# Local attention on one core: the last 512 rows loaded in order of use, and fourteen tiny extra loads

The kernel runs on 1 core of one Trainium2 chip. The metric is the device time of one execution in microseconds (us); the profile's span is some 1.8 us shorter than that time.

Words used below: PE does the matrix products (TensorE); ACT, DVE and POOL are ScalarE, VectorE and GpSimd; SP is SyncE, which here only issues transfers. A transfer (load or store) is issued by POOL or SP and carried out in packets by the 16 DMA engines. Each transfer adds sixteen increments to a semaphore, a counter that others wait on; it has landed when the last one has come. A ratio is a kernel's time over that of the kernel before, with its 95% interval in brackets.

## The reference

q, k and v are float32 of shape (4, 4096, 1536). Attention is taken inside windows of 64 rows.

```python
def reference(q, k, v):
    B, S, D = q.shape
    W = 64
    nw = S // W
    scale = D ** -0.5
    ...                                   # reshape to (B, nw, W, D)
    logits = np.einsum('bnwd,bnud->bnwu', q_w, k_w) * scale
    logits = logits - logits.max(axis=-1, keepdims=True)
    attn = np.exp(logits)
    attn = attn / attn.sum(axis=-1, keepdims=True)
    out = np.einsum('bnwu,bnud->bnwd', attn, v_w)
    return out.reshape(B, S, D).astype(np.float32)
```

There are 302 MB to read and 101 MB to write, and little arithmetic for them.

## The kernel before

The 16384 rows are cut into 32 units of 512 rows. The last unit is cut once more, into parts of 256, 128 and 128 rows, so that little work remains after the last load. Loads convert float32 to float16 and are issued from POOL, as are the stores. Only the first load of q and the last three stores come from SP.

```python
units = [Unit(i * UR, [(0, 4, 2)]) for i in range(N - 1)]
units.append(Unit((N - 1) * UR, [(0, 2, 2), (2, 3, 1), (3, 4, 1)]))
...
qkp = ctx.enter_context(tc.tile_pool(name="qkp", bufs=2))
vp = ctx.enter_context(tc.tile_pool(name="vp", bufs=3))
outp = ctx.enter_context(tc.tile_pool(name="outp", bufs=3))
...
def load(u, i, name):
    lo, hi, R = u.parts[i]
    ...                                   # take the tile, pick the rows
    nc.gpsimd.dma_start(out=dst, in_=rows(src, u.first[i], hi - lo, r))

def load_all(ui, names):
    if ui < N:
        for i in range(len(units[ui].parts)):
            for name in names:
                load(units[ui], i, name)
...
def store(u, i):
    lo, hi, R = u.parts[i]
    nc.gpsimd.dma_start(out=rows(of, u.first[i], hi - lo, R), in_=slots(u.o, lo, hi, R))

for ui, u in enumerate(units):
    for i in range(len(u.parts)):
        last = ui == N - 1 and i == len(u.parts) - 1
        blocks = scores(u, i)             # transposes of q and k on PE, products, exp
        if i == 0:
            load_all(ui + 2, "qk")
        for h, et in blocks:
            values(u, i, h, et, last)     # products with v, scaled; the last part stores itself
        if not last:
            store(u, i)
    load_all(ui + 3, "v")
```

So POOL issues four transfers a unit, always in the order q, k, out, v. Each full one has 3.15 MB on its 4-byte side. v of the last unit is issued before its q and k.

The softmax here doesn't subtract the row's maximum and nothing guards it: scores larger than these inputs give would overflow.

## Time and profile before

| | before |
|---|---|
| median time | 950.28 us (949.49 to 950.36, 3 runs) |
| span of the profiled execution | 948.6 us |
| PE, ACT, DVE busy | 70%, 46%, 45% |
| software DMA queue busy | 100.2% of 16 engines' span |
| landing to landing, one unit, steady state | 29.15 us |

From the page of the kernel before: busy time of each engine, and rows of the span in 40 slices (9 means 90% busy or more), then the DMA queue that holds nearly all bytes.

```profile
span 948.6 us, 12985 instructions
PE 666.8 (70%) x5624; PEld 443.1 (47%) x5624; DVE 426.9 (45%) x491; ACT 434.2 (46%) x612; POOL 83.7 (9%) x139
...
PE   2777776776767867767667677776776767777685
...
DMA  9999999999999999999999999999999999999997
...
q0 software_dynamic: 27232, 249.31, 100.2%
```

No compute engine is near full; the DMA engines are, in every slice but the last. Next, the list of DMA issues (count, KB, median us from issue to landing) and two lines of the list of waits (us in total, times, longest).

```profile
out_dram<-out_sb POOLq DMA_DIRECT2D x31, 3072.0 KB, 41.9
k<-in_k_dram POOLq DMA_DIRECT2D x31, 1536.0 KB, 48.6
v<-in_v_dram POOLq DMA_DIRECT2D x31, 1536.0 KB, 48.7
q<-in_q_dram POOLq DMA_DIRECT2D x30, 1536.0 KB, 53.8
...
```

```profile
POOL out_dram L224 <- issue: 376.6, 28, 14.4
...
PE tp L145 <- DMA k<-in_k_dram: 78.4, 28, 4.3
```

A full transfer takes 7.3 us of the queue, so a latency of 42 to 54 us means six or seven of them stand in line: the queue never lacks work. PE waits 2.8 us for k, 28 times.

What POOL does in steady state (timeline of POOL before: start, us, instruction, idle time before it and what ended that):

```profile
452.97 0.54 POOL L80 DMA_DIRECT2D q<-in_q_dram  x1 [1.34 <-PE tp L145]
463.05 0.54 POOL L80 DMA_DIRECT2D k<-in_k_dram  x1 [9.54 <-DVE xk L151]
476.80 0.71 POOL L224 DMA_DIRECT2D out_dram<-out_sb  x1 [13.21 <-issue]
477.51 0.72 POOL L80 DMA_DIRECT2D v<-in_v_dram  x1
```

POOL waits only for compute there. (The profile names nothing for the store's 13.21 us; that wait ended at 476.25 us, as DVE finished the last piece of the result.) At the end, PE meets the last unit at 918.9 us (timeline of PE before); neither line has a wait in brackets:

```profile
918.93 1.50 PE L145 MATMUL tp<-ident,q 128*128 128x128 f16 x24
920.53 1.20 PE L145 MATMUL tp<-ident,k 128*128 128x128 f16 x16
```

The trace also holds every increment of a DMA's semaphore, sixteen for each transfer. From these I computed when each transfer's first and last increment came. A growing distance between them says that some DMA engines run ahead of others: 0.7 us at 25 us, 9.1 us at 880 us. The trace doesn't name the engine.

### The profile page before, as it was taken

The numbers are of one execution on the slowest core, as the hardware profiler recorded it, in microseconds if no ns is written. First come the engines' busy times: TensorE is split into PE (matmuls) and PEld (weight loads), VectorE is DVE, ScalarE is ACT, GpSimd is POOL, SyncE is SP. The second block draws the span as 40 slices with busy tenths as digits, with TensorE's granted clock in tenths as the row PEclk, the third lists the DMA queues.
The fourth block names the chain that finished last, engine by engine and source line by source line (L and its number), as shares of the span: only waits on it lengthen the run. The fifth ranks groups of instructions, "written<-read, shape, count | busy, mean of one in ns | idle before, by whom it ended". The sixth has DMA issues, their size and how long they took to land. (4 is left out here: it accounts for less than half of the span.)

```text
span 948.6 us, 12985 instructions
## 1 busy us (share of the span) xinstructions
PE 666.8 (70%) x5624; PEld 443.1 (47%) x5624; DVE 426.9 (45%) x491; ACT 434.2 (46%) x612; POOL 83.7 (9%) x139
## 2 busy tenths in 40 slices
PE   2777776776767867767667677776776767777685
PEld 1544554444544545445454354544445534455452
DVE  3545445443454344543445443454434545344442
ACT  2555434444345444454534454435544445453444
POOL 1101110100101011010010100101101001011010
PEclk9999989888899889798988998989988999798798
DMA  9999999999999999999999999999999999999997
GB/s 259 215 234 262 282 280 280 247 253 279 281 278 252 246 282 282 279 263 242 278 281 279 271 241 271 282 279 275 242 263 282 281 277 253 254 279 281 279 258 312
DMA packets 27865, 254.07 MB, mean 268 GB/s; under 512 B 2208, under 2 KB 2208, under 8 KB 11808
## 3 DMA queue, kind: packets, MB, share of 16 engines
q0 software_dynamic: 27232, 249.31, 100.2%
q1 hardware_dynamic: 576, 3.93, 1.1%
q8 instruction: 44, 0.72, 0.3%
q14 instruction: 13, 0.11, 0.0%
HBM read 301.99 MB, written 100.66 MB: 424 GB/s over the span
## 5 line engine op out<-in xcount | busy, mean ns | idle before, releaser
L209 PE MATMUL o<-v,et 128*128 128x512 f16 x762 | 226.8, 402 | 65.6 <-ACT out_sb L215 61.4
L158 PE MATMUL lt<-xq,xk 128*128 128x256 f16 (+1 forms) x1536 | 236.9, 306 | 41.4 <-DVE xk L151 25.9
L151 ACT COPY xk<-tp 128x1024 f16<-128x1024 f16 (+1 forms) x96 | 123.6, 1287 | 255.8 <-PE tp L145 255.8
L217 DVE TENSOR_SCALAR out_sb<-o,rs 128x512 f32<-128x512 f32 x191 | 143.4, 751 | 161.7 <-PE o L209 161.7
L151 DVE COPY xk<-tp 128x1024 f16<-128x1024 f16 (+1 forms) x97 | 123.3, 1271 | 200.7 <-PE tp L145 200.7
L158 PEld LDWEIGHTS <-xk 128*128 128x128 f16 x1536 | 154.1, 110 | 92.3 <-DVE xk L151 39.0
L145 PE MATMUL tp<-ident,k 128*128 128x128 f16 x1536 | 136.4, 245 | 81.7 <-DMA k<-in_k_dram 78.4
L215 ACT ACTIVATE out_sb<-o,rs 128x512 f32<-128x512 f32 x193 | 132.7, 687 | 123.4 <-PE o L209 112.2
L145 PEld LDWEIGHTS <-k 128*128 128x128 f16 x1536 | 118.1, 112 | 94.1 <-DMA k<-in_k_dram 83.2
L209 PEld LDWEIGHTS <-et 128*128 128x128 f16 x762 | 72.7, 99 | 188.1 <-issue 147.5
L151 DVE COPY xq<-tp 128x1024 f16<-128x1024 f16 (+1 forms) x129 | 152.1, 1255 | 5.1 <-PE tp L145 5.0
L145 PE MATMUL tp<-ident,q 128*128 128x128 f16 x1536 | 103.0, 220 | 46.6 <-DVE xq L151 20.8
L145 PEld LDWEIGHTS <-q 128*128 128x128 f16 x1536 | 91.9, 98 | 64.6 <-issue 34.8
L151 ACT COPY xq<-tp 128x1024 f16<-128x1024 f16 x64 | 82.1, 1283 | 83.7 <-PE tp L145 83.7
L184 ACT ACTIVATE et<-lt,zeros 32x128 f16<-32x128 f32 (+1 forms) x256 | 91.8, 359 | 32.9 <-PE lt L158 27.4
L202 DVE RECIPROCAL rs<-sp 128x2 f32<-128x2 f32 (+1 forms) x65 | 10.7, 165 | 133.7 <-PE sp L197 133.7
L224 POOL DMA_DIRECT2D out_dram<-out_sb x33 | 23.2, 704 | 419.0 <-issue 376.6
L80 POOL DMA_DIRECT2D k<-in_k_dram x34 | 18.5, 546 | 352.1 <-PE tp L145 210.4
L197 PE MATMUL sp<-ones,et 128*128 128x1 f16 x254 | 16.0, 166 | 41.1 <-ACT et L184 41.1
L197 PEld LDWEIGHTS <-et 128*128 128x128 f16 x254 | 13.6, 98 | 60.0 <-ACT et L184 50.4
L80 POOL DMA_DIRECT2D q<-in_q_dram x33 | 17.9, 542 | 79.1 <-PE tp L145 58.8
L80 POOL DMA_DIRECT2D v<-in_v_dram x34 | 23.9, 703 | 4.9 <-DMA k<-in_k_dram 4.9
(12 smaller groups left out, 7.6 us busy)
## 6 DMA issues: line engine op xcount, KB each, us to landing
out_dram<-out_sb POOLq DMA_DIRECT2D x31, 3072.0 KB, 41.9
k<-in_k_dram POOLq DMA_DIRECT2D x31, 1536.0 KB, 48.6
v<-in_v_dram POOLq DMA_DIRECT2D x31, 1536.0 KB, 48.7
q<-in_q_dram POOLq DMA_DIRECT2D x30, 1536.0 KB, 53.8
raw<-in_q_dram SPq DMA_DIRECT2D x1, 3072.0 KB, 14.5
out_dram<-out_sb POOLq DMA_DIRECT2D x1, 1536.0 KB, 10.0
v<-in_v_dram POOLq DMA_DIRECT2D x1, 768.0 KB, 46.9
v<-in_v_dram POOLq DMA_DIRECT2D x2, 384.0 KB, 46.4
```

The source lines that it names most:

```text
L80: nc.gpsimd.dma_start(out=dst, in_=rows(src, u.first[i], hi - lo, r))
L145: nc.tensor.transpose(tp[:, (c - c0) * R + r, j, :], src[:, lo + R * j + r, c * P : (c + 1) * P], ident,)
L151: copy(out=dst, in_=tp)
L158: nc.tensor.matmul(lts[h][:, r, :, :], lhsT=kc[:, r, h, :], rhs=qc[:, :, h, :], start=(c == 0 and r == 0), stop=(c == DC - 1), skip_group_ ...
L184: nc.scalar.activation(et[s, :, :, s], lts[h][s, :, :, s], EXP, bias=zeros[s], scale=scale)
L197: nc.tensor.matmul(sp[:, t, 0:1], lhsT=et[:, r, t, :], rhs=ones[:, 0:1], start=(r == 0), stop=(r == R - 1),)
L202: nc.vector.reciprocal(out=rs, in_=sp[:, :, 0])
L209: nc.tensor.matmul(o, lhsT=et[:, r, t, :], rhs=u.v[:, lo + R * h + r, sl], start=(r == 0), stop=(r == R - 1),)
L215: nc.scalar.activation(dst, o, COPY, bias=0.0, scale=rs[:, t : t + 1])
L217: nc.vector.tensor_scalar_mul(dst, o, scalar1=rs[:, t : t + 1])
L224: nc.gpsimd.dma_start(out=rows(of, u.first[i], hi - lo, R), in_=slots(u.o, lo, hi, R))
```

## The change

The intent has two parts. The loads of the last 512 rows are issued in the order in which their parts are computed, so that the first part has all it needs earlier. And in fourteen units from the 15th on, one tiny load of 1 to 15 rows, whose result nobody reads, is put into the stream.

```diff
     def load_all(ui, names):
-        if ui < N:
-            for i in range(len(units[ui].parts)):
-                for name in names:
+        if ui < N - 1:
+            for name in names:
+                load(units[ui], 0, name)
+        elif ui == N - 1 and "q" in names:
+            for i, part in enumerate(("qkv", "qk", "qk")):
+                for name in part:
                     load(units[ui], i, name)
+            load(units[ui], 1, "v")
+            load(units[ui], 2, "v")
@@
+    probe = consts.tile([16, 192], FP32, name="probe")
     for ui, u in enumerate(units):
+        n = ui - 13
+        if 1 <= n <= 15 and n != 8:
+            w = 128 + 4 * n
+            nc.gpsimd.dma_start(out=probe[:n, :w], in_=qf[0:n, :w])
         for i in range(len(u.parts)):
```

In the diff, v of part 0 follows its q and k directly; v of parts 1 and 2 follow after all q and k.

## The prediction

> **What bounds the kernel.** The DMA engines, throughout. The page's DMA row is 9 in 39 of 40 slices and the software queue is busy 100.2% of 16 engines' span; PE is at 70%, ACT 46%, DVE 45%. Landing times (from the trace's semaphore records): in steady state every full load or store (3.15 MB on its 4-byte side) lands about 7.3 us after the one before, a unit of four (q, k, out, v) takes 29.15 us. Compute needs about 24.5 us from k's landing to the store; PE waits 78.4 us for k (list of waits). Issue to landing is 42 to 54 us (list of DMA issues): some 1.6 units stand in the queue.
>
> The end is DMA-bound too. The last load lands at 925.06 us, then the stores with no gap beyond their bytes: 932.40, 939.70, 943.35, 945.21, 945.85, 946.49, 947.13. The chain of waits shows compute from 926 to 944, but each result joins a queue that still holds older stores. The engines are not level: the first to finish a transfer leads the last by 0.7 us at 25 us and 9.1 us at 880 us, growing in jumps of about 1.1 us, near the 44 instruction fetches of 16 KB (about 0.9 us each). The slowest engine, never idle, sets the time.
>
> **What the change does.**
> 1. Last 512 rows: v came ahead of q and k; now each v follows its q and k. Same nine loads, same bytes. Before, part 0's k landed at 917.64 and PE reached that part at 918.7; q and k at about 910 and v at 914 buy nothing, since the slowest engine has the same work left. Last v lands near 925, its use is near 942. Worth 0.
> 2. Fourteen loads of 1 to 15 unused rows, 528 to 752 B a row. By the Trainium skill ("DMA: Bandwidth & Descriptors", why a DMA increments its semaphore by 16) n rows go to n engines and all 16 post the count; before has no such transfer. A 2048 B packet took 85 ns, a 4 B semaphore write 9 to 22 ns; splitting transfers at the end cost 0.02 to 0.06 us each beyond bytes. Estimate 0.035 us each, 0.5 us in all, on the critical DMA stream. Issuing costs POOL about 0.55 us each, hidden.
> 3. New waits on POOL. All probes write one tile, so each should wait for the one before to land; and transfers share eight semaphores in turn, so five a unit instead of four wait for a landing 1.6 units back. POOL should stand some 15 us at each probe; q's issue to landing falls from 53.9 to about 37 us in those units, k's to about 43; probes land in about 29 us. When the wait ends a whole unit (29 us; 20 on the engine furthest ahead) is still queued, so none runs dry: worth 0.
>
> **Predicted: 950.9 us**, range 949.2 to 953.0. Faster by over 2%: 0.01; within 2%: 0.97; slower: 0.02.
>
> **Right if** the DMA row stays 9, full transfers land 7.3 us apart, probes add under 0.1 us each, PE's wait for k is nearly unchanged, the last load lands near 925.5 and the end follows the stores. **Wrong if** POOL's waits run the queue dry (DMA row under 9 from 400 to 860 us, steps over 8 us): slower by up to some per cent; or if odd engine counts turn later transfers onto other engines that move at another rate, or level the lead (at most about 4 us faster); or if a fetch more or less falls on the slowest engine (1.1 us).

## The result, and the profile after

| | before | after |
|---|---|---|
| median time | 950.32 us (949.49 to 950.37, 4 runs) | 951.0 us (950.64 to 951.39, 4 runs) |
| ratio | | 1.0009, 95% interval 0.9992 to 1.0027 |
| span of the profiled execution | 948.6 us | 949.5 us |
| last load lands | 925.06 us | 925.59 us |
| last store lands | 947.13 us | 947.67 us |

A ratio is the mean time of one kernel's runs over that of the other's of the same rounds, so it is not quite the ratio of the medians in the table. The interval includes 1; the difference of 0.7 us is of the size predicted, but these runs alone don't separate it from nothing.

The page after:

```profile
span 949.5 us, 13010 instructions
PE 664.1 (70%) x5624; PEld 436.8 (46%) x5624; DVE 427.7 (45%) x491; ACT 433.8 (46%) x612; POOL 91.1 (10%) x153
...
PE   2777767677766876767677677675776667867675
...
DMA  9999999999999999999999999999999999999996
...
q0 software_dynamic: 27680, 249.38, 100.1%
```

Nothing has moved here: the DMA row is full as before. The list of DMA issues after, of the steady stretch from 400 to 800 us (thirteen or fourteen units), and two lines of the list of waits after, of the whole span:

```profile
out_dram<-out_sb POOLq DMA_DIRECT2D x13, 3072.0 KB, 42.6
k<-in_k_dram POOLq DMA_DIRECT2D x14, 1536.0 KB, 42.7
v<-in_v_dram POOLq DMA_DIRECT2D x13, 1536.0 KB, 49.1
q<-in_q_dram POOLq DMA_DIRECT2D x13, 1536.0 KB, 35.2
probe<-in_q_dram POOLq DMA_DIRECT2D x1, 0.5 KB, 48.6
probe<-in_q_dram POOLq DMA_DIRECT2D x1, 1.1 KB, 28.6
...
```

```profile
POOL probe L236 <- DMA probe<-in_q_dram: 214.8, 11, 21.3
...
PE tp L150 <- DMA k<-in_k_dram: 80.9, 28, 4.5
```

And POOL's timeline after, in the same part of the span as that shown of before:

```profile
469.98 0.53 POOL L236 DMA_DIRECT2D probe<-in_q_dram  x1 [20.28 <-DMA probe<-in_q_dram]
470.50 0.56 POOL L80 DMA_DIRECT2D q<-in_q_dram  x1
471.06 0.54 POOL L80 DMA_DIRECT2D k<-in_k_dram  x1
479.12 0.71 POOL L229 DMA_DIRECT2D out_dram<-out_sb  x1 [7.52 <-DVE out_sb L222]
479.83 0.72 POOL L80 DMA_DIRECT2D v<-in_v_dram  x1
```

This is a large new wait: 215 us in total in which POOL stands still. It ends when the small load of the unit before has landed. q is issued much later than before relative to its unit, so its issue-to-landing falls from some 54 us to 35 us, and k's from 49 to 43. But it lands when it would have landed anyway, because a whole unit of transfers still stood in the queue. PE's wait for k went from 78.4 to 80.9 us.

At the end (timeline of PE after), the last unit again starts without a wait, at 918.0 us:

```profile
918.03 1.50 PE L150 MATMUL tp<-ident,q 128*128 128x128 f16 x24
919.64 1.21 PE L150 MATMUL tp<-ident,k 128*128 128x128 f16 x16
```

The landings of the last 512 rows and of the stores behind them, from the semaphore records (last increment, us):

```
                       before     after
q, k, v of part 0      914.00 917.64 906.60    906.39 910.05 913.72
q, k, v of part 1      919.49 921.35 908.46    915.59 917.42 923.75
q, k, v of part 2      923.22 925.06 910.30    919.28 921.13 925.59
stores of units 30,31  932.40 939.70           932.91 940.23
stores of parts 0, 1   943.35 945.21           943.89 945.75
three stores of part 2 945.85 946.49 947.13    946.38 947.02 947.67
```

(Units are counted from 1 in this table.) The reorder did what it should: all of part 0 is there at 913.7 instead of 917.6 us. Nobody was waiting for it. The steps from store to store are the same to 0.03 us.

### The profile page after: what moved, and what is told of

Read it like the earlier page. It is cut to its first block, busy times and chain, and to the rows that moved or that the text cites. A ratio compares the mean times of both kernels' runs of the same rounds, so it can differ in the third digit from the quotient of the medians.

```text
span 949.5 us, 13010 instructions
## 1 busy us (share of the span) xinstructions
PE 664.1 (70%) x5624; PEld 436.8 (46%) x5624; DVE 427.7 (45%) x491; ACT 433.8 (46%) x612; POOL 91.1 (10%) x153
## 5 line engine op out<-in xcount | busy, mean ns | idle before, releaser
L214 PE MATMUL o<-v,et 128*128 128x512 f16 x762 | 232.4, 411 | 64.2 <-ACT out_sb L220 59.8
L163 PE MATMUL lt<-xq,xk 128*128 128x256 f16 (+1 forms) x1536 | 228.1, 298 | 39.8 <-DVE xk L156 24.7
L150 PE MATMUL tp<-ident,k 128*128 128x128 f16 x1536 | 133.1, 242 | 84.3 <-DMA k<-in_k_dram 80.9
L163 PEld LDWEIGHTS <-xk 128*128 128x128 f16 x1536 | 149.3, 107 | 88.8 <-DVE xk L156 40.7
L150 PEld LDWEIGHTS <-k 128*128 128x128 f16 x1536 | 115.3, 110 | 95.6 <-DMA k<-in_k_dram 85.7
L236 POOL DMA_DIRECT2D probe<-in_q_dram x14 | 7.4, 530 | 235.8 <-DMA probe<-in_q_dram 214.8
## 6 DMA issues: line engine op xcount, KB each, us to landing
k<-in_k_dram POOLq DMA_DIRECT2D x1, 768.0 KB, 35.2
```

The source lines that it names most:

```text
L150: nc.tensor.transpose(tp[:, (c - c0) * R + r, j, :], src[:, lo + R * j + r, c * P : (c + 1) * P], ident,)
L163: nc.tensor.matmul(lts[h][:, r, :, :], lhsT=kc[:, r, h, :], rhs=qc[:, :, h, :], start=(c == 0 and r == 0), stop=(c == DC - 1), skip_group_ ...
L214: nc.tensor.matmul(o, lhsT=et[:, r, t, :], rhs=u.v[:, lo + R * h + r, sl], start=(r == 0), stop=(r == R - 1),)
L236: nc.gpsimd.dma_start(out=probe[:n, :w], in_=qf[0:n, :w])
```

## The experiments

The main theory: the slowest of the 16 DMA engines never idles, so the order of loads and POOL's waits are worth nothing, and the small loads cost only what they add to that engine's stream. The rivals: that a gain of the reorder and a loss from the small loads cancel; that POOL's waits do cost; that compute sets the pace. "Before" ran again beside each set on the same chip; medians were 950.0 to 950.4 us.

### 1. Each half of the change alone: reorder_only and probes_only

reorder_only is the change without the tile and the small loads:

```diff
-    probe = consts.tile([16, 192], FP32, name="probe")
     for ui, u in enumerate(units):
-        n = ui - 13
-        if 1 <= n <= 15 and n != 8:
-            w = 128 + 4 * n
-            nc.gpsimd.dma_start(out=probe[:n, :w], in_=qf[0:n, :w])
```

probes_only is the kernel before with just these lines added.

> The change without the fourteen small loads. Main theory (the slowest DMA engine never idles, so the order of the last loads is worth nothing): 950.3 us, within 0.5 us of the kernel before; the last load lands near 925, q's issue-to-landing is back near 54 us, no new wait on POOL. Rival (the reorder gains and the small loads lose, and the two cancel in the change): 949 us or less, with probes_only at 952 or more.

Measured: 950.2 us (949.94 to 951.0, 5 runs), ratio 0.9998 (0.9986 to 1.0011). The last load landed at 924.69, q's median issue-to-landing was 53.9 us again, and POOL had no wait for a small load.

> The kernel before with the fourteen small loads, old order of the last loads. Main theory (about 0.03 to 0.05 us of DMA time for each small load, POOL's waits free): 950.8 us, 0.3 to 1.0 us over the kernel before, q's issue-to-landing near 36 us between 440 and 860 us. Rival (cancelling): 952 us or more.

Measured: 950.83 us (950.61 to 951.59, 5 runs), ratio 1.0005 (0.9993 to 1.0018). q's median issue-to-landing was 35.4 us from 440 to 860 us, as expected. No sign of two halves that cancel: neither differs from the kernel before by more than its interval, about 0.13% either way. The 0.5 us fits the small loads, but this run alone doesn't separate it from nothing either.

### 2. POOL's wait taken away: own_tiles

```diff
-    probe = consts.tile([16, 192], FP32, name="probe")
...
-            nc.gpsimd.dma_start(out=probe[:n, :w], in_=qf[0:n, :w])
+            own = consts.tile([16, 192], FP32, name=f"probe{n}")
+            nc.gpsimd.dma_start(out=own[:n, :w], in_=qf[0:n, :w])
```

> The change with a tile of its own for each small load, so that none waits for the one before it to land; the eight shared semaphores stay. Main theory (POOL's 15 to 20 us waits cost nothing): same as the change, 950.9 us, within 0.4 us; POOL's waits on the small loads are gone, q lands some 44 us after its issue. Rival (the waits cost something that the reorder hides): 0.6 us or more faster than the change.

Measured: 950.84 us (950.68 to 951.52, 5 runs), ratio 1.0005 (0.9992 to 1.0019). The small loads no longer wait for each other, and q lands 43.3 us after its issue. But POOL still waits for landings: 44 us in total before small loads (eleven waits for a k to land), 40 us before loads of q (six waits for a store) and 28 us before loads of k (four waits for a small load, which were expected to be gone); I take the shared semaphores to be the cause. So of 215 us about half came back as other waits; that some 100 us less of waiting changed nothing measurable is what this run shows. PE's wait for k was 76.5 us, against 78.4 us before and 80.9 us in the change.

### 3. What one small load costs: four_own_tiles

```diff
-    probe = consts.tile([16, 192], FP32, name="probe")
+    probes = [
+        [consts.tile([16, 192], FP32, name=f"probe{e}_{m}") for m in range(4)]
+        for e in range(2)
+    ]
...
-            nc.gpsimd.dma_start(out=probe[:n, :w], in_=qf[0:n, :w])
+            for m in range(4):
+                nc.gpsimd.dma_start(out=probes[n % 2][m][:n, :w], in_=qf[0:n, :w])
```

> The change with four small loads where it has one, on tiles that are used again two units later: 56 small loads. The landing times show a step of 0.17 us from a transfer to a small load behind it, but the transfer after it then comes after 7.10 instead of 7.28 us. Theory that a small load costs 0.03 to 0.04 us of DMA time: 56 x 0.035 = 2 us over the kernel before, 952.3 us. Rival, that each costs its 0.17 us step: 9.5 us, 959.8 us. DMA row 9 throughout in both.

Measured: 953.95 us (952.85 to 954.9, 5 runs), ratio 1.0035 (1.0022 to 1.0047). This lies between the two expectations and fits neither: some 3.3 us for 56 loads, by the means. So I looked for where the time was.

On the DMA engines: I took the engine that leads, because it shows none of the jumps, and measured from the landing of v of one unit to that of v fourteen units later. That took 408.31 us before and in reorder_only; 408.46, 408.61 and 408.54 us in the change, probes_only and own_tiles, with 13 small loads between; and 409.28 us here, with 52. So a small load costs about 0.019 us of DMA time here, (409.28 − 408.31)/52. Three more kernels bear on it: last_stores_sp and tail_reversed (below), which have no small loads, took 408.30 us too; four_last_sp (below), with the same 52 between, took 408.99 us, which is 0.013 us each. The step of 0.17 us to its own landing is no cost; the next transfer makes it up. That is about 0.7 to 1 us for 56.

The rest is after the last landing. The program ends with a drain instruction on POOL, and in the kernel before that is what the end waits for: it ends at 947.79 us, 0.66 us after the last landing of all, while SP is done at 947.28. Its distance from POOL's own last landing grows with the number of transfers that POOL has issued (the last three rows are runs told below):

```
                  transfers   POOL's last   drain      distance
                  from POOL   landing, us   ends, us   us
before               134        945.21       947.79      2.58
reorder_only         134        944.86       947.44      2.58
tail_reversed        134        945.88       948.46      2.58
extra_loads          142       1002.51      1005.42      2.91
the change           148        945.75       948.78      3.03
probes_only          148        945.39       948.42      3.03
own_tiles            148        945.61       948.64      3.03
pairs_one_tile       162       1026.18      1029.66      3.48
four_own_tiles       190        945.60       949.93      4.33
last_stores_sp       132        944.67       947.18      2.51
four_last_sp         188        944.58       948.84      4.26
all_stores_sp        101        942.55       943.46      0.91
```

That is 0.031 to 0.032 us for each added small load ((4.33 − 2.58)/56), more than what it costs on the DMA engines. In the change it makes 0.45 us. It isn't one price for every transfer: the eight full loads of extra_loads added 0.041 us each, and all_stores_sp, with 33 stores fewer on POOL, saved 0.051 us for each. In all, the span after the last landing grew from 1.42 us before to 3.48 us here, by 2.06 us; with 0.7 to 1 us on the DMA engines that is near the 3.3 us measured.

### 4. The closing drain put out of the way: last_stores_sp and four_last_sp

```diff
     def store(u, i):
         lo, hi, R = u.parts[i]
-        nc.gpsimd.dma_start(out=rows(of, u.first[i], hi - lo, R), in_=slots(u.o, lo, hi, R))
+        queue = nc.sync if u is units[-1] else nc.gpsimd
+        queue.dma_start(out=rows(of, u.first[i], hi - lo, R), in_=slots(u.o, lo, hi, R))
```

The first is this edit on the kernel before, the second on four_own_tiles.

> The kernel before, with the first two stores of the last 512 rows issued from SP instead of POOL. In the profiles so far POOL's closing drain ends 2.58 us after POOL's last transfer lands with 134 transfers from POOL, 3.03 with 148, 3.48 with 162, 4.33 with 190: about 0.032 us for each; in the kernel before it ends 0.66 us after the last landing of all and is what the end waits for. Theory: POOL's last landing is now near 939.7, its drain is over near 942.5 and hidden, the span ends about 0.9 us after the last landing instead of 1.4: 0.5 us less, 949.9 us. Rival (the drain waits for the end of the program whatever POOL's last transfer): no change.

Measured: 949.7 us (949.47 to 950.85, 5 runs), ratio 0.9998 (0.9986 to 1.0011). The time can't tell. The trace can: POOL's drain ended at 947.18 us, before SP was done (947.90), so it no longer ended the program, and the span ended 0.90 us after the last landing instead of 1.42. One detail was wrong: POOL's last landing was at 944.67 and not 939.7, because the stores from SP's queue overtook the store that POOL had issued earlier.

> The kernel with 56 small loads (four_own_tiles: 953.95 us, ratio 1.0035) with the same two stores issued from SP. If most of the cost of the small loads is POOL's closing drain (4.33 us after its last landing), which is now hidden behind the last stores: 2 to 2.3 us faster than four_own_tiles, 951.5 us, ratio near 1.001; what is left is the time of the small loads on the DMA engines, 0.02 us each. Rival (the cost lies on the DMA engines): ratio stays near 1.0035.

Measured: 951.93 us (950.41 to 952.62, 5 runs), ratio 1.0016 (1.0003 to 1.003), against 1.0035 for four_own_tiles. By the ratios, moving two stores to another queue took back about 1.8 us (0.19% of 950 us), but the two intervals overlap. The traces are clearer: the span after the last landing is 2.19 us against 3.48 us in four_own_tiles, 1.29 us less; the same edit took 0.52 us (1.42 to 0.90) from the kernel before, which has no small loads. The drain still ended last here, at 948.84 us, so not all of it was hidden. Together with last_stores_sp this supports the drain as the larger part of the cost. What the drain does in that time no record shows.

### 5. Where POOL's wait would cost: pairs_one_tile

```diff
-            nc.gpsimd.dma_start(out=probe[:n, :w], in_=qf[0:n, :w])
+            for m in range(2):
+                nc.gpsimd.dma_start(out=probe[:n, :w], in_=qf[0:n, :w])
```

> The change with each small load issued twice in a row on the one tile, so the second waits for the first to land while nothing stands behind it: the queue runs dry fourteen times. Wrong on purpose in nothing; results stay correct. Main theory (a wait of POOL costs only when the queue empties): at each pair the slowest engine idles about 1.5 to 3 us and the lead of the other engines (up to 9 us) is lost, so 2.5 to 4 us a pair, 985 to 1006 us, 990 likely; the DMA row shows 8 or less in slices of 450 to 870 us. Rival (only the number of small loads counts): 14 more loads at 0.035 us, 951.5 us.

Measured: 1033.09 us (1032.2 to 1033.24, 4 runs), ratio 1.087 (1.0855 to 1.0885). The rival is out by 80 us. The mechanism is the expected one. The DMA row of its page, and POOL's timeline around one pair:

```profile
DMA  9999999999999999997889889999898899889897
```

```profile
507.57 0.55 POOL L237 DMA_DIRECT2D probe<-in_q_dram  x1
539.63 0.52 POOL L237 DMA_DIRECT2D probe<-in_q_dram  x1 [31.52 <-DMA probe<-in_q_dram]
540.14 0.56 POOL L80 DMA_DIRECT2D q<-in_q_dram  x1
540.69 0.56 POOL L80 DMA_DIRECT2D k<-in_k_dram  x1
541.22 0.74 POOL L229 DMA_DIRECT2D out_dram<-out_sb  x1
```

The wait of 31.5 us is only one and a half times the 20 us of the change, but at its end the queue is empty. Busy time and DMA share (the last two columns: mean share of the 16 engines, GB/s) in three stretches of that cycle: while the second small load is alone, until q lands, until k lands:

```profile
539.35:541.22 1.87, 1.02 (x4) 0.38 (x4) 0.49 (x2) 1.16 (x3) 1.59 (x4) 1.00 0.03 5
541.22:551.19 9.97, 4.67 (x20) 1.60 (x19) 3.83 (x6) 3.00 (x5) 1.96 (x4) 0.86 1.01 196
551.19:560.13 8.94, 4.65 (x48) 4.32 (x48) 4.95 (x4) 2.58 (x2) 0.00 (x0) 0.69 1.00 249
```

The size was wrong: 82 us for 14 pairs, 5.9 us each, where I had 2.5 to 4. I had counted the idle time and the lost lead. I had not counted that q and k after a restart are slow: in the pair shown they land 9.97 and 8.94 us after what came before, instead of 7.3. Over the fourteen restarts, with packets taken in order of their start, the first sixteen packets of q took 1.57 us on average and the last 48 of k 1.23 us; those between took 0.93 us, as nearly all load packets do in the change. On average the second small load landed 2.06 us after the first, q 9.28 us after that and k 8.58 us after q, which is 5.4 us more than two steps of 7.28 us and so most of the 5.9 us. Why these packets are slower stays open.

### 6. An order of loads that does matter: tail_reversed

```diff
-            for i in range(len(units[ui].parts)):
+            for i in reversed(range(len(units[ui].parts))):
```

> The kernel before with the last 512 rows loaded in the reverse order of use: part 2, part 1, part 0. Part 0's k then lands last, near 925 us, where PE wants it at 918.7 us: compute of the end shifts by 6.4 us, more than the slack of the last stores (1 to 6 us). Main theory: the order of loads counts only beyond that slack, so about 956 us (954 to 958), and the last stores no longer land back to back. Rival (bytes alone count, order never): 950.3 us.

Measured: 953.4 us (952.37 to 954.61, 5 runs), ratio 1.0033 (1.002 to 1.0046). Order does count beyond the slack, but by half of what I expected. Timeline of PE at the start of part 0:

```profile
921.33 2.74 PE L145 MATMUL tp<-ident,q 128*128 128x128 f16 x24 [3.33 <-DMA q<-in_q_dram]
924.97 1.07 PE L145 MATMUL tp<-ident,k 128*128 128x128 f16 x16 [0.89 <-DMA k<-in_k_dram]
```

PE first reads k at 920.53 us in the kernel before, so it was 4.4 us late at 924.97, not 6.4 us: I had compared k's landing with PE's arrival at q. The last store was issued 3.4 us later than before (947.49 against 944.09) and landed 2.6 us later (949.73 against 947.13). The stores no longer landed back to back: store of part 1 after 2.68 us instead of 1.86, the next after 2.55 instead of 0.63.

### 7. More bytes: extra_loads

```diff
+    extra = consts.tile([P, SLOTS, D], FP16, name="extra")
     for ui, u in enumerate(units):
+        if ui in (14, 16, 18, 20, 22, 24, 26, 28):
+            nc.gpsimd.dma_start(out=slots(extra, 0, SLOTS, SLOTS), in_=rows(qf, 0, SLOTS, SLOTS))
```

> The kernel before with one more full load (3.15 MB read, unused) in each of eight units from 14 to 28. If DMA bounds every unit: 8 x 7.29 = 58.3 us more, 1008.6 us. Rival (compute sets the unit's 29.15 us and DMA has room to spare up to it): under 25 us more.

Measured: 1008.62 us (1007.95 to 1009.88, 4 runs), ratio 1.0619 (1.0602 to 1.0635). Each extra load of 3.15 MB cost 7.3 us, all of its DMA time. Compute doesn't set the pace.

### 8. All stores from SP: all_stores_sp

```diff
-        nc.gpsimd.dma_start(out=rows(of, u.first[i], hi - lo, R), in_=slots(u.o, lo, hi, R))
+        nc.sync.dma_start(out=rows(of, u.first[i], hi - lo, R), in_=slots(u.o, lo, hi, R))
```

> The kernel before with every store issued from SP, 101 transfers from POOL left. Same bytes on the same engines: if bytes on the slowest engine set the time, only the closing drain's 0.5 us goes: 949.8 us (949.2 to 950.4). If stores from another queue overtake loads and PE then waits longer for k at the end, slower; if they move at another rate, off by several us either way.

Measured: 959.01 us (955.55 to 959.24, 5 runs), ratio 1.0086 (1.0072 to 1.0099). The main expectation was wrong, and the two named exceptions came true. The profile was taken in its fastest run. There the stores overtook the loads: a full store landed 21.3 us after its issue instead of 41.9. The Trainium skill ("DMA: Bandwidth & Descriptors", Queues, rings and completion order) says that each DMA engine takes turns between the queues it has work for; this agrees. The loads came later for it. The k of the second to last unit landed at 904.96 us instead of 895.62, PE began the last unit at 926.3 instead of 918.9 us, and the last store landed at 952.66. The stores were also slower: a 12,288 B packet of a store took 472 ns on average, against 461.5 ns in the kernel before; loads' packets of that size took 926 against 930 ns. The time of all packets, divided by 16 engines, was 966.7 us against 963.4 us: some 3.4 us, out of the 5.5 us by which the last store was later. So the late loads are not shown to be the main cause; no run separates the two. What the order of landings does show is that one queue keeps the stores behind the loads that the end needs.

No experiment points to a version that clearly beats both kernels. last_stores_sp is the best by its trace, and its time can't be told from that of before.

## Why the prediction was right

- **The bound.** Right, and shown: extra_loads cost its full DMA time, 7.3 us each, and pairs_one_tile shows what an idle queue costs. That the jumps of the lead come from instruction fetches was argued from their times and sizes and was not tested.
- **Reorder worth 0.** Right: reorder_only 0.9998. tail_reversed shows why the question was a fair one: the same nine loads in another order cost 3 us, once a load comes later than its use by more than the stores' slack.
- **Small loads 0.5 us.** The sum was right: 0.5 us in probes_only and own_tiles, 0.7 us in the change, although each value has an uncertainty of about a microsecond. The place was partly wrong. I put "0.5 us in all, on the critical DMA stream". On the DMA engines they cost some 0.2 to 0.3 us (14 × 0.013 to 0.019), and 0.45 us came from POOL's closing drain, which I had not looked at. The estimate of 0.035 us each, taken from split transfers, was too high for the engines by a factor of two or so. That both errors compensate is luck.
- **New waits on POOL.** Right in mechanism: I said about 15 us at each small load, 37 us for q, 43 us for k and 29 us for a small load; the profile has 18 to 21 us at twelve of the fourteen, 35.2, 42.7 and mostly 28.6 us. The other two (n = 1 and 9) have no small load in the unit before, so nothing held them up; they took 49 and 50 us to land. Worth 0: right, as far as own_tiles shows it.
- **"n rows go to n engines".** The trace has exactly n packets of the load's row size for each n from 2 to 15 (n = 8 has no load), and for n = 15 they start at 15 different distances, up to 8.5 us, from the first: that fits one row on each of 15 engines. For n = 1 it was wrong: twelve packets of 44 B, so the one row had been split. The section that I had named allows for it: a contiguous single row may be cut into the largest factor of its length up to 16, and 12 is that factor of 132 values.
- **What would make it wrong.** None of it happened: no dry queue, no other rate (full transfers still 7.3 us apart), no change of the lead beyond a microsecond (9.1 us before, 8.7 us after, near 880 us).

## What to carry to other kernels

Before moving a load earlier, ask whether anyone waits for it: read the landing of the load and the start of its first use, and see whether the queue behind it stays full. A wait of an issuing engine is worth what the queue loses by it: 20 us were free while a unit of transfers stood in line, and a wait of 31 us cost 6 us once nothing did. At the end of a program look past the last transfer too: closing instructions can be the last link, and their length can depend on how much was issued.

## What the Trainium skill lacked or had wrong

- No page that I read has a closing drain on POOL that grows with what POOL issued. It ended 2.58 us after POOL's last landing with 134 transfers issued, 3.03 with 148, 4.33 with 190: about 0.03 us for each added small load, on the critical path here. It belongs to "DMA: Bandwidth & Descriptors", section SWDGE vs HWDGE vs iDMA.
- "DMA: Bandwidth & Descriptors", section Anatomy of one DMA, gives a fixed cost of about 2.0 us for a DMA. A small load alone on an empty queue took 1.6 to 2.3 us from issue to its last increment (fourteen in pairs_one_tile, median 1.75), which agrees. In a full queue one added 0.013 to 0.019 us. The page lacks the second number, which is the one that counts where DMA is the bound.
- The same page, on how many engines a DMA uses (Why a DMA increments its semaphore by 16), says that a load on k < 16 engines takes k consecutive ones from a moving cursor, with an exception for some direct copies. For 9 and for 10 rows the packets start at nearly the same distances from the first (both have 0.83, 1.35, 1.63, 2.48, 2.91 us), and so it is up to 13 rows, though a cursor would have sent them to mostly different engines. That fits the exception and not the cursor. The trace doesn't name engines, so this is an inference.
- "Runtime: NRT & Kernel Launch", section Instruction fetch mechanics, calls the cost of crossing a 16 KiB block mostly hidden. The trace has 44 such fetches of 0.88 to 0.98 us each on single DMA engines, and the engines drift 9 us apart in jumps of about 1.1 us near them. In a kernel that is bound by DMA they are probably not hidden; no run here tested it.
- No page that I read has the slow restart: after an empty queue the first sixteen packets of q took 1.57 us on average and the last 48 of k 1.23 us, against 0.93 us for those between (pairs_one_tile).
